# The up product of a two-layer MLP in seven block products instead of eight

## The chip, the cores and the metric

The program runs on one core of a Trainium2 chip. The core has TensorE (PE in the profile, with its weight loads as PEld), VectorE (DVE), ScalarE (ACT), GpSimd (POOL) and SyncE (SP, which issues the DMA transfers). The metric is the device time of one execution in microseconds (us). The kernel before took 2497.71 us, the median of three runs from 2495.82 to 2503.09.

## The reference

Two blocks of two layers each work on 512 tokens of 1024 features in float32. Only the second half of each layer of the first block is touched by the change:

```python
def hybrid_layer(x, ...):
    ...                                   # attention part
    x = x + mixed @ w_out
    h = rms_norm(x, mlp_norm_w)           # x / sqrt(mean(x^2) + eps) * mlp_norm_w
    return x + jnp.square(jax.nn.relu(h @ w_up)) @ w_down
```

`w_up` is 1024 x 4096 and `w_down` 4096 x 1024, one of each per layer; the first block has two layers. After it come a final norm and the second block (a forgetting attention, a linear recurrence and two gated MLPs), which stay as they are.

## The kernel before

Everything is held with features on the 128 partitions and the 512 tokens along the free axis: `x` is eight tiles of 128x512. A product in float32 accuracy is made of three matmuls in the rounded type fp32r (`mm3`, lines 321 to 323): each operand is split into a high part `hi`, which ScalarE makes by rounding, and a low part `lo`, the rest, which VectorE or GpSimd makes by subtraction; then hi x hi, hi x lo and lo x hi are added up in PSUM. A weight tile of 128 output features by 1024 input features comes by one DMA of 512 KB into a `raw` buffer (`load`, line 257), is rounded into `whi` (line 268) and subtracted into `wlo` (line 269). There are three buffers of each of the three. `fm_tiles` (line 329) makes one or more output tiles of 128x512: 8 chunks of the input x 3 matmuls of 512 columns, with the first six chunks of several tiles interleaved and the last two tile by tile.

The MLP (`mlp`, line 858) begins with `pre_norm`: the eight tiles `xg`, which are x times the norm's weight, split into high and low parts (lines 314, 315), and the squares of x (line 400) added up on VectorE (line 406). The factor 1/sqrt(mean square) of each token, `rstd`, is made on GpSimd (line 437), spread over the partitions as `rb`, and multiplied into the result of the up product rather than into its input. The squares take temporaries of the tag "t", of which there are four.

`up` makes the activation tiles: relu and the token's factor in one VectorE instruction out of PSUM (line 866), the square on ScalarE (867), the high part on ScalarE (275) and the low part on GpSimd (276). `down` makes the eight output tiles from eight activation tiles and adds them to x (874). A layer has 32 up tiles and 32 down products of eight chunks, in four groups of eight (`groups`, line 878): the first three up tiles together, five more, then for each group two up tiles of the next group, the eight down tiles, and six more up tiles.

The kernel is written in a framework that tracks dependencies and buffers. Each engine has one queue in a fixed order. The order is settled beforehand by a planner that gives every engine, by its own cost estimates, the first instruction in program order that is ready and has a free buffer; so an instruction can be moved ahead of ones written before it. The buffers of the MLP lie in a pool of their own, opened by `phase` in `hybrid`, over the addresses of the attention part.

Of the kernel before, what the change touches and what calls it, by code (L numbers as in the profile page):

```python
# [8 lines left out]
F = mybir.dt.float32  # L9
R = mybir.dt.float32r  # L10
B = mybir.dt.bfloat16
AF = mybir.ActivationFunctionType
OP = mybir.AluOpType
AX = mybir.AxisListType

S = 512
# [144 lines left out]
class Net:  # L161
# [183 lines left out]
    def catch_up(self):  # L345
# [2 lines left out]
            f()  # L348
        self.later = []

    def tm_half(self, ps, h, src, acts, width, low=None):


        if h == 0:
            ps = [self.mm_tile() for _ in range(NB)]
        w = self.weights(src, 4 * width, low)
        for tb in range(NB):
            ts = slice(tb * 128, (tb + 1) * 128)
            for k in range(4):
                sl = slice(k * width, (k + 1) * width)  # L360
                a = acts[4 * h + k]
                self.mm3(ps[tb][:, :width], (a[0][:, ts], a[1][:, ts]), (w[0][:, sl], w[1][:, sl]),
                         h == 0 and k == 0, h == 1 and k == 3)
        return ps
# [207 lines left out]
    def hybrid(self, l):  # L572
        with self.phase(act=10, lo=4, v=2, o=1, pr=2, ph=2, pl=2, score=1, gt=2):
            self.mixers(l)
        with self.phase(act=20):
            self.mlp(l)

    def mixers(self, l):
# [279 lines left out]
    def mlp(self, l):  # L858
        nc, I, x = self.nc, self.I, self.x
        xg, _, rb = self.pre_norm("mlp_norm", l)  # L860

        def up(js):
            out = []
            for ps in self.fm_tiles([(self.weights(I["w1up"][l, j], 1024, nc.vector), 0) for j in js], xg):
                t, s = self.temp(), self.temp()
                nc.vector.scalar_tensor_tensor(t, ps, 0.0, rb, op0=OP.max, op1=OP.mult)  # L866
                nc.scalar.activation(s, t, AF.Square)
                out.append(self.split(s, nc.gpsimd))
            return out

        def down(g, acts):
            for j in range(8):
                ps = self.fm_tile(self.weights(I["w1down"][l, g, j], 1024, nc.vector), acts)
                nc.vector.tensor_add(x[j], x[j], ps)  # L874

        self.groups([8] * 4, up, down)

    def groups(self, sizes, up, down, ahead=2, together=3):

# [410 lines left out]
```

## Time and profile before

| what | value |
|---|---|
| median of three runs | 2497.71 us |
| the profiled execution | 2494.83 us |
| its span | 2493.0 us |
| TensorE busy | 2404.7 us (96%), 11217 matmuls |
| VectorE, ScalarE, GpSimd busy | 1360.7 (55%), 1039.4 (42%), 619.0 (25%) us |
| granted TensorE clock, mean | 0.992 |
| DMA | 215.30 MB, mean 86 GB/s |

Busy time of TensorE is not the same as TensorE at its peak, as matmuls overlap: one of 512 columns is shown with some 0.4 us, while the next one starts some 0.23 us after it. The distance between starts is the better measure of what a matmul costs. The busy time of VectorE and GpSimd holds what an instruction waits for after it has started.

### The profile page before, as it was taken

How to read it: one execution, taken by the hardware profiler on the slowest of the kernel's cores; microseconds unless marked ns; L12 is line 12 of the kernel's file. 1: busy time of each engine (PE TensorE's matmuls, PEld its weight loads, DVE VectorE, ACT ScalarE, POOL GpSimd, SP SyncE). 2: the span in 40 equal slices, each digit the busy share in tenths (PEclk: the TensorE clock that was granted, in tenths of full speed). 3: DMA queues.
4: the chain of work that ended last, by engine and by line, in shares of the span. 5: the costliest groups of instructions: out<-in, count | busy, mean ns of one | idle time of the engine just before them, and what ended most of it. 6: DMA issues, size and time to landing. Idle time of an engine off the chain costs nothing.

```text
span 2493.0 us, 29049 instructions
## 1 busy us (share of the span) xinstructions
PE 2404.7 (96%) x11217; PEld 1950.8 (78%) x11217; DVE 1360.7 (55%) x2217; ACT 1039.4 (42%) x1625; POOL 619.0 (25%) x435
## 2 busy tenths in 40 slices
PE   9899999999998999999999999999999989999997
PEld 7787788888877878888887886888886766888886
DVE  6978643333488786333347867333336765433334
ACT  5656642232365675332233564223223563322222
POOL 3465320011045742110112531100001542100101
PEclk9999999999999999999999999999999999999998
DMA  4311132222232112222222211222222322322221
GB/s 160 106 64 47 64 102 93 95 100 93 77 104 91 60 47 86 100 93 93 93 97 77 84 52 60 97 98 94 93 83 70 95 75 68 102 96 98 94 87 66
DMA packets 61513, 215.30 MB, mean 86 GB/s; under 512 B 6848, under 2 KB 6976, under 8 KB 61376
## 3 DMA queue, kind: packets, MB, share of 16 engines
q1 hardware_dynamic: 59760, 207.06, 25.0%
q0 software_dynamic: 1472, 6.29, 0.7%
q8 instruction: 88, 1.44, 0.2%
q14 instruction: 49, 0.40, 0.1%
q10 hardware_dynamic: 144, 0.11, 0.0%
HBM read 211.33 MB, written 2.10 MB: 86 GB/s over the span
## 4 chain that ended last, share of the span: by engine, by line
PE 78%; DVE 14%; ACT 4%; issue 3%; POOL 1%; DMA 0%; ACTq 0%; DVEq 0%; POOLq 0%
PE mm L323 24%; PE mm L322 24%; PE mm L321 24%; DVE x L946 1%; DVE score L647 1%; PE st L307 1%; DVE m L646 1%; PE st L308 1%; PE st L542 1%; DVE m L1143 1%; ACT xg L314 1%; DVE act L287 1%; PE av L416 1%; DVE hs L1172 1%; PE av L491 1%
## 5 line engine op out<-in xcount | busy, mean ns | idle before, releaser
L268 ACT ACTIVATE whi<-raw 128x1024 fp32r<-128x1024 f32 (+3 forms) x398 | 409.8, 1032 | 1116.7 <-PE mm L322 934.6
L323 PE MATMUL mm<-xg,wlo 128*128 128x512 f32 x1792 | 711.5, 398 | 1.7 <-DVE wlo L269 1.7
L321 PE MATMUL mm<-xg,whi 128*128 128x512 f32 x1792 | 699.1, 394 | 14.3 <-ACT xg L314 12.1
L322 PE MATMUL mm<-xg,whi 128*128 128x512 f32 x1792 | 711.3, 397 | 0.2
L321 PE MATMUL mm<-act,whi 128*128 128x512 f32 x1160 | 455.8, 395 | 11.4 <-ACT act L275 8.5
L322 PE MATMUL mm<-act,whi 128*128 128x512 f32 x1160 | 459.8, 397 | 1.4 <-POOL act L276 1.4
L323 PE MATMUL mm<-act,wlo 128*128 128x512 f32 x1160 | 460.3, 397 | 0.0
L276 POOL TENSOR_TENSOR act<-t,act 128x512 fp32r<-128x512 f32 x108 | 150.4, 1395 | 1105.6 <-ACT act L275 1077.3
L269 DVE TENSOR_TENSOR wlo<-raw,whi 128x1024 fp32r<-128x1024 f32 (+2 forms) x289 | 348.4, 1207 | 135.8 <-ACT whi L268 135.3
L321 PEld LDWEIGHTS mm<-xg,whi 128*128 128x128 f32 x1792 | 339.5, 190 | 99.1 <-ACT xg L314 20.3
L322 PEld LDWEIGHTS mm<-xg,whi 128*128 128x128 f32 x1792 | 337.1, 188 | 82.9 <-DVE xg L315 6.6
L323 PEld LDWEIGHTS mm<-xg,wlo 128*128 128x128 f32 x1792 | 336.7, 188 | 76.2 <-DVE wlo L269 4.1
L269 POOL TENSOR_TENSOR wlo<-raw,whi 128x1024 fp32r<-128x1024 f32 (+3 forms) x109 | 257.3, 2362 | 296.0 <-ACT whi L268 284.7
L321 PEld LDWEIGHTS mm<-act,whi 128*128 128x128 f32 x1160 | 220.4, 190 | 64.6 <-ACT act L275 10.9
L322 PEld LDWEIGHTS mm<-act,whi 128*128 128x128 f32 x1160 | 218.3, 188 | 54.3 <-DVE act L276 2.3
L323 PEld LDWEIGHTS mm<-act,wlo 128*128 128x128 f32 x1160 | 218.1, 188 | 47.4
L874 DVE TENSOR_TENSOR x<-x,mm 128x512 f32<-128x512 f32 x64 | 44.0, 688 | 206.2 <-PE mm L323 206.2
L866 DVE SCALAR_TENSOR_TENSOR t<-mm,rb 128x512 f32<-128x512 f32 x64 | 44.1, 691 | 198.8 <-PE mm L323 198.6
L1237 DVE TENSOR_TENSOR t<-mm,rb 128x512 f32<-128x512 f32 x44 | 30.4, 691 | 141.8 <-PE mm L323 141.8
L1235 DVE TENSOR_TENSOR t<-mm,rb 128x512 f32<-128x512 f32 x44 | 30.4, 691 | 118.1 <-PE mm L323 118.1
L275 ACT ACTIVATE act<-t 128x512 fp32r<-128x512 f32 x114 | 72.1, 633 | 50.2 <-DVE t L1238 32.9
L307 PE MATMUL st<-act,act 128*128 128x128 f32 (+3 forms) x208 | 72.2, 356 | 20.8 <-DVE act L287 8.8
(226 smaller groups left out, 2641.5 us busy)
## 6 DMA issues: line engine op xcount, KB each, us to landing
raw<-in_w1up SPq DMA_DIRECT2D x64, 512.0 KB, 3.3
raw<-in_w1down SPq DMA_DIRECT2D x64, 512.0 KB, 3.2
raw<-in_gate SPq DMA_DIRECT2D x44, 512.0 KB, 3.3
raw<-in_up SPq DMA_DIRECT2D x44, 512.0 KB, 3.2
raw<-in_w1fm SPq DMA_DIRECT2D x41, 512.0 KB, 3.3
raw<-in_down SPq DMA_DIRECT2D x32, 512.0 KB, 3.2
raw<-in_odin SPq DMA_DIRECT2D x16, 512.0 KB, 3.3
raw<-in_w1out SPq DMA_DIRECT2D x16, 384.0 KB, 3.0
```

The costliest lines, as they stand in the source:

```text
L268: nc.scalar.activation(hi[:, sl], raw[:, sl], AF.Copy)
L269: (low or nc.gpsimd).tensor_sub(lo[:, sl], raw[:, sl], hi[:, sl].bitcast(F))
L275: nc.scalar.activation(hi, t, AF.Copy)
L276: (low or nc.vector).tensor_sub(lo, t, hi.bitcast(F))
L307: mm(ps, a[:, rows], b[hh][:, cols], start=True, stop=False, skip_group_check=True)
L321: mm(ps, w[0], a[0], start=first, stop=False, skip_group_check=True)
L322: mm(ps, w[0], a[1], start=False, stop=False, skip_group_check=True)
L323: self.last_mm = mm(ps, w[1], a[0], start=False, stop=last, skip_group_check=True)
L866: nc.vector.scalar_tensor_tensor(t, ps, 0.0, rb, op0=OP.max, op1=OP.mult)
L874: nc.vector.tensor_add(x[j], x[j], ps)
L1235: nc.vector.tensor_mul(t, pg, rb)
L1237: nc.vector.tensor_mul(u, pu, rb)
```

## The change

In the MLPs of the first block, 26 of the 32 up tiles of a layer are made in 13 pairs. A pair is 256 output features by 512 tokens by 1024 inputs. It is cut in two along each of the three: the features (two tiles), the inputs (chunks 0 to 3 and 4 to 7) and the tokens (0 to 255 and 256 to 511). The product of two 2x2 block matrices is formed of seven block products and a number of block sums, where the plain way has eight. The sums of token blocks (`token_sums`) are made once a layer, those of weight blocks (`pair_weights`) once a pair, both on GpSimd, and both are split into high and low parts as other operands are. A block product is 4 chunks x 3 matmuls of 256 columns. `seven` runs in three parts: three products, then two, then two; the last part of a pair is put behind the first part of the next pair, or behind the first down tile. Two of the PSUM tiles are read after the first part and are added to further. What follows the up product (relu, factor, square, split) is done for the two tiles of a pair from SBUF. Tiles 0 to 3, 30 and 31 are made as before.

The pool of the MLP holds 10 activation tiles in place of 20, and the tiles of the sums. The descriptor memory for transfers that GpSimd issues is halved.

```diff
+    def token_sums(self, x, g):
+        nc, out = self.nc, []
+        for k in range(4):
+            b = [self.temp() for _ in range(2)]
+            for i in range(2):
+                nc.scalar.activation(b[i], x[k + 4 * i], AF.Copy, scale=g(k + 4 * i))
+            (b11, b12), (b21, b22) = [(t[:, :256], t[:, 256:]) for t in b]
+            f = self.get("sum", 2 * S)
+            t1, t2, t3, t4 = [f[:, 256 * i:256 * i + 256] for i in range(4)]
+            nc.gpsimd.tensor_sub(t1, b12, b11)
+            nc.gpsimd.tensor_sub(t2, b22, t1)
+            nc.gpsimd.tensor_sub(t3, b22, b12)
+            nc.gpsimd.tensor_sub(t4, b21, t2)
+            t = self.get("tok", 4 * S, R)
+            hi, lo = t[:, :2 * S], t[:, 2 * S:]
+            nc.scalar.activation(hi, f, AF.Copy)
+            nc.vector.tensor_sub(lo, f, hi.bitcast(F))
+            out.append((hi, lo))
+        return out
+
+    def pair_weights(self, src):
+        nc = self.nc
+        r0, r1 = (self.load(a, 1024) for a in src)
+        (a11, a12), (a21, a22) = [(r[:, :S], r[:, S:2 * S]) for r in (r0, r1)]
+        def parts(t, width, tags):
...
+            nc.scalar.activation(hi[:, :width], t, AF.Copy)
+            nc.vector.tensor_sub(lo[:, :width], t, hi[:, :width].bitcast(F))
+            return hi, lo
+        a1 = parts(r0[:, :1024], 1024, ("whi", "wlo"))
+        p, q = self.get("sum", 2 * S), self.get("sum", 2 * S)
+        s1, s2, s3, s4 = p[:, :S], p[:, S:], q[:, :S], q[:, S:]
+        nc.gpsimd.tensor_add(s1, a21, a22)
+        nc.gpsimd.tensor_sub(s2, s1, a11)
+        s12 = parts(p, 1024, ("shi", "slo"))
+        nc.gpsimd.tensor_sub(s3, a11, a21)
+        nc.gpsimd.tensor_sub(s4, a12, s2)
+        s34 = parts(q, 1024, ("shi", "slo"))
+        a2 = parts(a22, 512, ("whi", "wlo"))
+        return a1, s12, s34, a2
+
+    def seven(self, src, xg, tok, post):
...
+        def product(ps, w, j, b, first):
+            for k in range(4):
+                sl = slice(512 * j + 128 * k, 512 * j + 128 * k + 128)
+                self.mm3(ps, (w[0][:, sl], w[1][:, sl]), b(k), first and k == 0, k == 3)
+        p1, p2, p3 = (t[:, :256] for t in (self.mm_tile(), self.mm_tile(), self.st_tile()))
...
+        product(p1, a1, 0, plain(0, 0), True)
+        product(p2, s12, 1, summed(1), True)
+        product(p3, s12, 0, summed(0), True)
+        nc.scalar.activation(r1, p1, AF.Copy)
+        nc.vector.tensor_add(r2, p2, r1)
+        yield
+        t, u = self.temp(), self.temp()
+        product(p1, a1, 1, plain(1, 0), False)
+        product(p2, s34, 0, summed(2), False)
+        nc.scalar.activation(t[:, half[0]], p1, AF.Copy)
+        nc.vector.tensor_add(r3, p2, r1)
+        nc.vector.tensor_add(u[:, half[1]], p3, r3)
+        yield
+        product(p2, a2, 0, summed(3), False)
+        product(p3, s34, 1, plain(1, 1), False)
+        nc.vector.tensor_add(u[:, half[0]], p2, r1)
+        nc.vector.tensor_add(t[:, half[1]], p3, r2)
+        post(t, u)
+        yield
...
-        with self.phase(act=20):
+        with self.phase(act=10, tok=4, sum=2, shi=3, slo=3, r=2):
             self.mlp(l)
...
+        def both(j):
+            def post(*tu):
+                for i, t in enumerate(tu):
+                    nc.vector.scalar_tensor_tensor(t, t, 0.0, rb, op0=OP.max, op1=OP.mult)
+                    nc.scalar.activation(t, t, AF.Square)
+                    acts[j + i] = self.split(t, nc.gpsimd)
+            return self.seven([I["w1up"][l, j + i] for i in range(2)], xg, tok, post)
...
+        def pairs(js):
+            for j in js:
+                now = both(j)
+                next(now)
+                finish()
+                next(now)
+                left.append(now)
+
+        def finish():
+            while left:
+                next(left.pop())
+
+        up(range(3))
+        tok = self.token_sums(x, lambda c: self.v("mlp_norm", 8 * l + c))
+        up([3])
+        pairs([4, 6])
+        for g in range(4):
+            if g < 3:
+                pairs([8 * g + 8])
+            down(g, 0)
+            finish()
+            for j in range(1, 8):
+                down(g, j)
+            if g < 2:
+                pairs(range(8 * g + 10, 8 * g + 16, 2))
+            elif g == 2:
+                pairs([26, 28])
+                up([30])
+                finish()
+                up([31])
...
-    nc = _bacc.Bacc("TRN2", target_bir_lowering=False, num_devices=1, dynamic_dma_scratch_size=8192)
+    nc = _bacc.Bacc("TRN2", target_bir_lowering=False, num_devices=1, dynamic_dma_scratch_size=4096)
```

## Rows read from the trace of the kernel before

**Rows 1.** The page: busy time by engine, and the chain that ended last.
```profile
PE 2404.7 (96%) x11217; PEld 1950.8 (78%) x11217; DVE 1360.7 (55%) x2217; ACT 1039.4 (42%) x1625; POOL 619.0 (25%) x435
...
PE 78%; DVE 14%; ACT 4%; issue 3%; POOL 1%; DMA 0%; ACTq 0%; DVEq 0%; POOLq 0%
```

**Rows 2.** Windows: length, busy by engine (instructions), clock, DMA share, GB/s.
```profile
180.00:240.00 60.00, 55.71 (x295) 45.49 (x293) 52.45 (x132) 42.00 (x87) 34.39 (x28) 1.00 0.13 43
340.00:660.00 320.00, 320.00 (x1381) 260.26 (x1380) 117.14 (x126) 101.46 (x125) 38.27 (x32) 1.00 0.28 94
```

**Rows 3.** Waits from 309 to 666 us: total us, times, longest.
```profile
ACT whi L268 <- PE mm L322: 217.8, 58, 8.2
...
DVE t L866 <- PE mm L323: 99.3, 29, 3.5
```

**Rows 4.** Timeline, TensorE: first matmul of one up tile and of the next.
```profile
411.18 0.39 PE L321 MATMUL mm<-xg,whi 128*128 128x512 f32 x1
...
416.73 0.39 PE L321 MATMUL mm<-xg,whi 128*128 128x512 f32 x1
```

**Rows 5.** Timeline, TensorE: matmuls of 256 columns, 43 starts apart.
```profile
159.96 0.28 PE L323 MATMUL mm<-whi,xg 128*128 128x256 f32 x1
...
164.99 0.28 PE L321 MATMUL mm<-whi,xg 128*128 128x256 f32 x1
```

**Rows 6.** Groups by form, VectorE: count, busy us, mean ns, idle before.
```profile
L269 DVE TENSOR_TENSOR wlo<-raw,whi 128x1024 fp32r<-128x1024 f32 x264 | 324.4, 1230 | 123.1 <-ACT whi L268 122.6
...
L1238 DVE TENSOR_TENSOR t<-t,t 128x512 f32<-128x512 f32 x44 | 30.4, 692 | 5.6 <-ACT t L1236 1.7
...
L547 DVE TENSOR_TENSOR pl<-st,ph 128x256 fp32r<-128x256 f32 x32 | 13.2, 413 | 1.8 <-ACT ph L546 1.8
```

**Rows 7.** Groups by form, ScalarE.
```profile
L268 ACT ACTIVATE whi<-raw 128x1024 fp32r<-128x1024 f32 x351 | 371.1, 1059 | 1031.5 <-PE mm L322 874.4 <-issue 138.8 <-PE mm L323 6.5
...
L867 ACT ACTIVATE t<-t 128x512 f32<-128x512 f32 x64 | 40.4, 632 | 2.8 <-DVE t L866 2.5 <-issue 0.2
...
L546 ACT ACTIVATE ph<-st 128x256 fp32r<-128x256 f32 x32 | 12.3, 385 | 0.0
```

**Rows 8.** Groups by form, GpSimd.
```profile
L406 POOL TENSOR_TENSOR acc<-acc,t 128x512 f32<-128x512 f32 x15 | 19.5, 1299 | 42.0 <-ACT t L400 42.0
...
L276 POOL TENSOR_TENSOR pl<-t,ph 128x256 fp32r<-128x256 f32 x8 | 7.0, 876 | 11.9 <-ACT ph L275 11.7
```

**Rows 9.** Timeline, VectorE and GpSimd: an add alone and beside GpSimd.
```profile
2097.65 0.68 DVE L946 TENSOR_TENSOR x<-x,m 128x512 f32<-128x512 f32 x1
2103.04 1.80 DVE L946 TENSOR_TENSOR x<-x,m 128x512 f32<-128x512 f32 x1
2103.00 1.29 POOL L406 TENSOR_TENSOR acc<-acc,t 128x512 f32<-128x512 f32 x1 [1.97 <-ACT t L400]
```

**Rows 10.** Timeline, VectorE and GpSimd, at the first layer's MLP start.
```profile
316.23 3.08 DVE L406 TENSOR_TENSOR acc<-acc,t 128x512 f32<-128x512 f32 x4
...
333.46 0.69 DVE L866 SCALAR_TENSOR_TENSOR t<-mm,rb 128x512 f32<-128x512 f32 x1 [2.25 <-PE mm L323]
320.97 1.04 POOL L437 TENSOR_TENSOR rstd<-var,mhalf 128x4 f32<-128x4 f32 x1 [26.12 <-DVE var L422]
331.23 3.81 POOL L276 TENSOR_TENSOR act<-t,act 128x512 fp32r<-128x512 f32 x3 [9.23 <-ACT act L275]
```

**Rows 11.** Windows and TensorE's timeline around one idle time (clock third from last).
```profile
128.00:134.00 6.00, 5.56 (x26) 5.57 (x27) 5.49 (x12) 2.30 (x5) 1.38 (x2) 0.50 0.26 90
...
128.44 1.11 PE L719 MATMUL st<-const_sb,t 128*128 128x128 f32 x4 [3.38 <-DVE t L713]
```

**Rows 12.** DMA issues: a transfer that GpSimd issues (count, KB, us to landing).
```profile
pr<-in_decay POOLq DMA_DIRECT2D x8, 640.0 KB, 4.7
```

More of the change, by code (lines that the diff above doesn't have):

```diff
@@ new lines, in pair_weights @@
+    def pair_weights(self, src):
[3 more added lines that the diff above has]
+        def parts(t, width, tags):
+            pool = self.wp if tags[0] == "whi" else self.pool
+            kw = {} if tags[0] == "whi" else {"bufs": self.bufs[tags[0]]}
+            w = 1056 if tags[0] == "whi" else 1024
+            hi, lo = (pool.tile([128, w], R, tag=tag, name=self.name(tag), **kw) for tag in tags)
+            nc.scalar.activation(hi[:, :width], t, AF.Copy)
[12 more added lines that the diff above has]
+        return a1, s12, s34, a2
@@ new lines, in seven, with plain, summed @@
+    def seven(self, src, xg, tok, post):
+        nc = self.nc
+        a1, s12, s34, a2 = self.pair_weights(src)
+        half = (slice(0, 256), slice(256, 512))
+        def plain(j, i):
+            return lambda k: tuple(part[:, half[i]] for part in xg[4 * j + k])
+        def summed(i):
+            return lambda k: tuple(part[:, 256 * i:256 * i + 256] for part in tok[k])
+        def product(ps, w, j, b, first):
[3 more added lines that the diff above has]
+        p1, p2, p3 = (t[:, :256] for t in (self.mm_tile(), self.mm_tile(), self.st_tile()))
+        r = self.get("r", 768)
+        r1, r2, r3 = (r[:, 256 * i:256 * i + 256] for i in range(3))
+        product(p1, a1, 0, plain(0, 0), True)
[17 more added lines that the diff above has]
+        yield
@@ L860, in mlp @@
         xg, _, rb = self.pre_norm("mlp_norm", l)
-        def up(js):
[L863 to L874, printed above, removed]
@@ L876, in mlp, with squared @@
-        self.groups([8] * 4, up, down)
+        acts = {}
+        def squared(j, ps):
+            t = self.temp()
+            nc.vector.scalar_tensor_tensor(t, ps, 0.0, rb, op0=OP.max, op1=OP.mult)
+            nc.scalar.activation(t, t, AF.Square)
+            acts[j] = self.split(t, nc.gpsimd)
+        def up(js):
+            for j, ps in zip(js, self.fm_tiles([(self.weights(I["w1up"][l, j], 1024, nc.vector), 0) for j in js], xg)):
+                squared(j, ps)
+        def both(j):
+            def post(*tu):
+                for i, t in enumerate(tu):
+                    nc.vector.scalar_tensor_tensor(t, t, 0.0, rb, op0=OP.max, op1=OP.mult)
+                    nc.scalar.activation(t, t, AF.Square)
+                    acts[j + i] = self.split(t, nc.gpsimd)
+            return self.seven([I["w1up"][l, j + i] for i in range(2)], xg, tok, post)
@@ new lines, in down @@
+        def down(g, j):
+            ps = self.fm_tile(self.weights(I["w1down"][l, g, j], 1024, nc.vector), [acts[8 * g + k] for k in range(8)])
+            nc.vector.tensor_add(x[j], x[j], ps)
+        left = []
+        def pairs(js):
[9 more added lines that the diff above has]
+        up(range(3))
```

## The prediction

> **What bounds the kernel now.** I read the page's busy times and its chain first, then the MLP stage by windows, then the waits in it, then single instructions. The reader is to see that TensorE is busy for 96% of the span and makes 78% of the chain that ended last [rows 1]. In the MLP stage of the first layer TensorE is busy for 320.00 of 320 us at full clock, while VectorE works 117, ScalarE 101 and GpSimd 38 of them [rows 2]. The waits agree: there ScalarE's weight copies wait for TensorE to release a weight buffer, 58 times and 218 us in all, and VectorE's evacuations wait for the last matmul of their tile [rows 3]; TensorE has no wait in this stage. So a matmul column taken away here shortens the time until another engine fills its place, and the whole question is how far the three others, at 12 to 37% now, can be loaded.
>
> **The matmuls.** A tile of the up product is 8 chunks x 3 matmuls of 512 columns. One tile's 24 matmuls start 411.18 to 416.73, 5.55 us, 231 ns each [rows 4]; a pair of tiles costs 11.10 us. In the new form a pair is 7 products x 4 chunks x 3 matmuls = 84, of 256 columns. The trace has that pattern already, twelve matmuls of 256 columns to a bank, each with its own 128x128 weight load, in the value projections of the mixers: 43 starts from 159.96 to 164.99 [rows 5] are 117.0 ns each, hardly over half of 231. That makes 84 x 0.117 = 9.83 us, 1.27 us less a pair, and over 13 pairs x 2 layers **33.1 us less**. The new products have the weights stationary and tokens moving, those of the row the other way round; shapes and types are the same, so I take the price unchanged.
>
> The Trainium skill (TensorE: Matmul & The Clock Gate, section Back-to-back issue gap) gives 518 cycles for 512 columns and 262 for 256. By those figures, as an estimate, the saving would be 30.9 us; the trace's pitches are longer, 231 and 117 ns, and they decide.
>
> **What is added per pair.** By the forms of [rows 6 to 8]:
> - ScalarE: three 1024-wide roundings at 1.059 in place of two, and a 512-wide one at 0.632; two 256-wide copies out of PSUM at 0.385; the four squares and roundings at 0.632 stay. 7.1 us of 9.83 (before 4.6 of 11.10).
> - VectorE: three 1024-wide subtractions at 1.23, one of 512 at 0.69, five 256-wide adds out of PSUM at 0.413, two relu-scalings at 0.692. 7.8 us (before 3.8).
> - GpSimd: four 512-wide weight sums at 1.30 and the two low parts at 1.27 (3.81 for three [rows 10]). 7.7 us (before 2.5).
>
> Each alone fits beside 9.83 us of matmuls. Together they fit less well, because GpSimd and VectorE exclude each other in some instructions: the add x + m takes 0.68 alone and 1.80 when it starts 0.04 us after a 1.29 us GpSimd add [rows 9], about the rest of that and its own time. Only VectorE instructions with both operands in SBUF meet this; the evacuation beside a GpSimd one keeps its 0.69 [rows 10]. Per pair the instructions that exclude each other are GpSimd's 7.7 and VectorE's subtractions and relu-scalings, 4.4 + 1.4: **13.5 us against 9.83**. That is no bound by itself, as pairs come in stretches of four (10, 12, 14, 16) between eight down tiles of 5.55 us, whose only such work is one subtraction of 1.23. In those the buffers let the first pair's weights be made whole (5.2 + 4.4) and the second's sums and first rounding (5.2 + 1.2), 16.0 us ahead. Of the stretch's 54 us, 16.0 are thus done and 4.0 (the last pair's relu and low parts) come after it: 34 us fall in 39.3 us of matmuls. It fits with an eighth to spare, with queues in a fixed order. The cost of the collisions lies between nothing (the 0 of the MLP stage, VectorE at 37%) and the 7.1% that TensorE stands idle at 180 to 240 us, where VectorE is busy at 87% [rows 2]: 0 to 0.70 us a pair, 18 us in all at the upper end. That stretch is attention, where TensorE hangs on VectorE inside each head, while here a weight buffer lies ready ahead; I take 0.25, **6.5 us over 26 pairs**.
>
> **The beginning of each layer's MLP.** Here nothing can be done ahead. The token sums need all of x, and their scaled copies take the four "t" temporaries that the squares of the norm still hold: those are released by the adds that end at 316.23 + 3.08 = 319.3 [rows 10], the first about 317, so GpSimd can begin at about 318. From there the work of GpSimd, and of VectorE where it excludes GpSimd, before the first pair's second product is: 16 subtractions of 128x256, between half of 1.27 and the 0.876 of that form [rows 8], taken as 0.75, 12.0 us; their four low parts at 1.23, 4.9; the rstd power on GpSimd, 1.0 [rows 10]; the low parts of tile 3's and the pair's own weights, 2.5; s1 and s2, 2.6. That is 23.0, to 341.0, and then a rounding and a subtraction, 2.3: 343.3. TensorE leaves tile 3 at 333.46 [rows 10] and has one product of 1.4 us without sums, so it stands at 334.9, 8.4 us early. The scheduler can bring forward products of plain tokens, the pair's other one and one of the next pair, 2.8 us; 5.6 us of idling remain. One idle of 3.38 us in this trace dropped the granted clock to 0.50, the 1.2 GHz level, through 128 to 134 us [rows 11], where a 256-column matmul then needs twice the time: some 2.8 us more. Together 8.4 us a layer, **16.8 us for two**. Ends: 0, if the sums hide; 8.4 + 3.8 + 2.8 = 15.0, if the first three tiles' low parts (3.81, GpSimd) stand before the sums and nothing is brought forward.
>
> **Edits costed at nothing.** r2, r3 and the halves are read out of PSUM while other products run: after part one of a pair comes the previous pair's last part (2.8 us) or a product of a1, against 0.41 or 0.39 for the read; without that cover 0.4 to 0.8 us once a group. The first down tile after a pair needs that pair's two activations at its chunks 6 and 7, 2.8 + 18 x 0.231 = 7.0 us after the pair's last matmul; add, relu 0.69 twice, square and two roundings 0.63, low part 1.27 twice are 5.3 us; without cover up to 2 us, 6 times. The weight loads (two a pair, as before) wait on SP for a raw buffer, now held for four sums: 5.2 us, inside the pair's 9.83. Half the descriptor memory of the GpSimd queue touches 12 transfers in the mixers, 8 of them of 640 KB that land in 4.7 us [rows 12]. If each of the 8 waited for the one before it and all stood on the path, that would be 38 us; I take nothing, since no wait of TensorE in the profile is on them and they are few in the air at once.
>
> **Sum.** -33.1 + 6.5 + 16.8 = -9.8 us. The profiled execution took 2494.83 us (span 2493.0, 1.8 around it): 2485.0. It lies 2.9 below the median of the three runs; from that it would be 2487.9. I forecast 2486.
>
> **Rivals.**
> - *All of it hides* (22%). For it: GpSimd is idle for 26.1 us before 320.97 [rows 10]; the two sum engines may take their work in another order than I walked. Against: the temporaries. Start 0 to 2 us a layer and 0.1 us a pair: -33.1 + 4 = -29, 2466.
> - *The start eats it* (20%). The low parts of tiles 0 to 2 are older work and stand ahead of the sums, and the clock falls: 15 us a layer. -33.1 + 30 + 6.5 = +3, 2498.
> - *The shared access becomes the bound in the stretches* (15%, slower). Place: the four-pair stretches; price 13.5 us a pair instead of 9.83. With no work ahead, 26 x (13.5 - 11.10) = +62. If half of the 16 us in each of six stretches is had ahead, +62 - 48 + 16.8 = +31, 2526. It decides from 9.83 + (33.1 - 16.8) / 26 = 10.5 us a pair. For it: whi, shi and raw have three buffers and a pair takes two of each, so work ahead may be little. Against: the walk above. The Trainium skill (SBUF — State Buffer, Who interferes with whom) has this rule: a VectorE instruction with two SBUF inputs and a GpSimd one that reads SBUF hold a shared access by turns, whole instructions long, and the second to come is blocked fully. The trace agrees by the 1.80 against 0.68.
> - *256 columns cost more here* (3%). A pair breaks even at 11.10 / 84 = 132 ns a matmul; the row says 117.
>
> **How the numbers follow.** My own case has 40%, at 2486, from 2478 to 2494. This kernel's timing can tell 0.3%, 7.5 us, from no change: under 2490 is faster, over 2505 slower. Faster: 22 + 35 of my 40 = 57%. Same: 17 of the start's 20, 5 of mine and 3 of the third rival's 15, 25%. Slower: the other 12, the fourth's 3 and 3 of the start's, 18%. The range takes the first rival nearly whole and leaves out the worse half of the third: 2463 to 2508.
>
> **What would show it.** The 256-column matmuls of the up product start 117 ns apart in a stretch, and one layer's stage shortens by 16.5 less its idling. TensorE's waits gain a line at the first pair of each layer, on the low part of the first weight sums, 5 to 12 us, with a clock of 0.50 after it. GpSimd rises to about 120 us a layer, and VectorE's subtractions average over 1.4 us where they meet it. I am wrong if TensorE waits more than 0.6 us a pair inside the stretches, or if the start has no such wait.

## The result, and the profile after

The changed kernel takes 2538.68 us (median of four runs, 2531.17 to 2540.32) against 2500.40 for the kernel before beside it: a ratio of **1.0149, 95% interval 1.0122 to 1.0176**. It is slower by 1.5%, and 31 us above the upper end of my range.

From here on each layer's MLP is cut at three marks: the last of the attention part's adds to x, the first down product's add to x, and the last one. These rows give them for the first layer, first of the kernel before, then of the changed one (line, engine, operation, output and inputs, count: shortest/median/longest ns, first and last start).

```profile
L856 DVE TENSOR_TENSOR x<-x,mm x8: 681/682/687, 301.8 to 309.5; 128x512 f32<-128x512 f32 x8
L874 DVE TENSOR_TENSOR x<-x,mm x32: 686/687/689, 372.4 to 667.5; 128x512 f32<-128x512 f32 x32
```

```profile
L948 DVE TENSOR_TENSOR x<-x,mm x8: 681/685/689, 302.3 to 310.0; 128x512 f32<-128x512 f32 x8
L975 DVE TENSOR_TENSOR x<-x,mm x32: 673/686/690, 394.3 to 685.8; 128x512 f32<-128x512 f32 x32
```

The *start* (first mark to second) was 372.4 - 309.5 = 62.9 us and is 84.3. The *body* (second to third) was 295.1 and is 291.5. The second layer gives the same: 63.0 and 295.1 before, 84.4 and 292.8 after. So the bodies are 5.9 us shorter in all and the starts 42.8 longer. The profiled executions differ by 45.3 us (span 2538.3 against 2493.0); the rest is the attention part of the second layer, 309.4 against 301.3. Its code is the same, and over the profiled executions of this study it took 299.5 to 309.4, so I don't count it to the change; the 309.4 itself stays unexplained.

The page after, answering to [rows 1]: busy times, then the chain of waits by engine. TensorE's share of the chain has fallen from 78% to 71% and GpSimd's risen from 1% to 4%; GpSimd's busy time is 181 us longer.

```profile
PE 2393.1 (94%) x12153; PEld 1987.9 (78%) x12153; DVE 1480.7 (58%) x2407; ACT 1108.0 (44%) x1753; POOL 800.1 (32%) x571
PE 71%; DVE 15%; issue 4%; ACT 4%; POOL 4%; DMA 1%; SPq 0%; POOLq 0%; ACTq 0%; DVEq 0%
```

TensorE's waits in the first layer's MLP, 310 to 690 us (engine, line, releaser: us in total, times, longest). In the kernel before this view is empty.

```profile
PE mm L321 <- ACT r L426: 17.0, 1, 17.0
PE mm L323 <- DVE wlo L387: 3.4, 2, 1.7
PE mm L321 <- ACT shi L386: 2.5, 2, 2.3
PE mm L321 <- DVE r L427: 2.1, 1, 2.1
PE mm L323 <- DVE slo L387: 0.8, 1, 0.8
```

The second line lies in the body, the other four, 22.4 us, at the start. Windows of TensorE there (stretch, PE busy and count, granted clock, DMA share, GB/s):

```profile
330.00:340.00 10.00, 5.31 (x29) 0.89 0.00 1
340.00:350.00 10.00, 0.00 (x0) 0.50 0.00 0
350.00:360.00 10.00, 7.48 (x39) 0.59 0.06 10
360.00:370.00 10.00, 4.81 (x31) 0.92 0.55 187
370.00:380.00 10.00, 10.00 (x79) 0.90 0.16 50
```

TensorE stands still from 335.3 to 352.3. When it starts again the clock is at 0.50, the 1.2 GHz level, and the 256-column matmuls come 0.21 us apart instead of 0.12; over the whole start that, and the first matmul behind each wait, is some 5 us more. The next three fences show the standstill: GpSimd, ScalarE and TensorE of the changed kernel (start, us, instruction, [idle before it and what ended it]).

```profile
321.49 1.04 POOL L529 TENSOR_TENSOR rstd<-var,mhalf 128x4 f32<-128x4 f32 x1 [26.12 <-DVE var L514]
330.98 0.74 POOL L363 TENSOR_TENSOR sum<-t 128x256 f32<-128x256 f32 x1 [8.45 <-ACT t L359]
331.68 3.92 POOL L276 TENSOR_TENSOR act<-t,act 128x512 fp32r<-128x512 f32 x3
335.55 0.73 POOL L364 TENSOR_TENSOR sum<-t,sum 128x256 f32<-128x256 f32 x1
...
349.68 0.72 POOL L366 TENSOR_TENSOR sum<-t,sum 128x256 f32<-128x256 f32 x1
350.36 1.27 POOL L393 TENSOR_TENSOR sum<-raw 128x512 f32<-128x512 f32 x1
```

```profile
324.58 1.06 ACT L268 ACTIVATE whi<-raw 128x1024 fp32r<-128x1024 f32 x1 [8.15 <-PE mm L322]
...
330.20 0.71 ACT L359 ACTIVATE t<-x,vec_sb 128x512 f32<-128x512 f32 x1
...
334.39 0.73 ACT L359 ACTIVATE t<-x,vec_sb 128x512 f32<-128x512 f32 x1 [0.27 <-POOL act L276]
...
346.60 1.06 ACT L369 ACTIVATE tok<-sum 128x1024 fp32r<-128x1024 f32 x1 [1.59 <-POOL sum L366]
350.43 1.06 ACT L369 ACTIVATE tok<-sum 128x1024 fp32r<-128x1024 f32 x1 [2.77 <-POOL sum L366]
351.39 0.61 ACT L958 ACTIVATE t<-t 128x512 f32<-128x512 f32 x1
351.91 0.36 ACT L426 ACTIVATE r<-mm 128x256 f32<-128x256 f32 x1
```

```profile
352.33 0.58 PE L321 MATMUL mm<-xg,whi 128*128 128x256 f32 x1 [17.02 <-ACT r L426]
```

Read them in this order. GpSimd is free from 322.5, and waits 8.45 us for the first scaled copy of x (line 359), which ScalarE makes only at 330.20. The copy needs a temporary "t". All four were free by 319.8, when the norm's last add ends, but a tag's buffers are handed out in the order of the program, and the results of tiles 0 to 2 (`up(range(3))`) are written ahead of the copies: three of the four went to them, and those can't be filled before rb exists. The copy at 334.39 says it: it waits for a low part of an activation (line 276), which frees a temporary. The first copy has the fourth temporary and waits for no buffer. It stands in ScalarE's queue behind a weight rounding that waited 8.15 us for TensorE (324.58), behind rb and behind a first square; why the planner put it there the trace doesn't show. GpSimd makes the three low parts of tiles 0 to 2 (3.92) in between, then the sums until 350.4. ScalarE, in its fixed order, waits for them four times, and behind those waits stands the read of the pair's first product, r1 (line 426, 0.36 us), on which TensorE waits.

The 17.0 us are not what r1 costs, though. The first matmul with a token sum starts at 355.03, only 2.7 us after TensorE goes on, so an earlier r1 would have moved the standstill more than shortened it. The chain that ended last doesn't pass through r1; it stays with GpSimd for most of the time from 330.98 to 366. Pieces of it (start, us, what):

```profile
330.98 0.74 POOL sum L363
...
341.50 1.06 ACT tok L369
342.56 0.62 ACT t L359
343.25 1.17 POOL sum L363
...
356.13 2.22 POOL sum L396
358.37 3.44 DMA raw<-in_w1up
361.98 1.28 POOL sum L393
```

At its end GpSimd waits for the weights of the next pair, whose load starts only when a buffer that the sums read is free.

### The profile page after: what moved, and what is told of

It is laid out like the page before. It is cut to its first block, busy times and chain, and to the rows that moved or that the text cites. A ratio compares the mean times of both kernels' runs of the same rounds, so it can differ in the third digit from the quotient of the medians.

```text
span 2538.3 us, 31459 instructions
## 1 busy us (share of the span) xinstructions
PE 2393.1 (94%) x12153; PEld 1987.9 (78%) x12153; DVE 1480.7 (58%) x2407; ACT 1108.0 (44%) x1753; POOL 800.1 (32%) x571
## 4 chain that ended last, share of the span: by engine, by line
PE 71%; DVE 15%; issue 4%; ACT 4%; POOL 4%; DMA 1%; SPq 0%; POOLq 0%; ACTq 0%; DVEq 0%
PE mm L323 21%; PE mm L322 21%; PE mm L321 21%; DVE x L1078 1%; PE st L307 1%; DVE score L739 1%; PE st L308 1%; DMA raw<-in_w1up 1%; DVE m L738 1%; POOL act L276 1%; DVE m L1275 1%; PE st L634 1%; DVE act L287 1%; PE st L321 1%; PE st L322 1%
## 5 line engine op out<-in xcount | busy, mean ns | idle before, releaser
L268 ACT ACTIVATE whi<-raw 128x1024 fp32r<-128x1024 f32 (+3 forms) x346 | 354.8, 1028 | 872.7 <-PE mm L322 681.1
L321 PE MATMUL mm<-xg,whi 128*128 128x512 f32 (+1 forms) x1584 | 598.6, 383 | 47.4 <-ACT r L426 34.0
L323 PE MATMUL mm<-xg,wlo 128*128 128x512 f32 (+1 forms) x1584 | 607.7, 384 | 9.2 <-DVE wlo L387 7.1
L322 PE MATMUL mm<-xg,whi 128*128 128x512 f32 (+1 forms) x1584 | 608.0, 384 | 0.2
L276 POOL TENSOR_TENSOR act<-t,act 128x512 fp32r<-128x512 f32 x108 | 155.9, 1453 | 758.1 <-ACT act L275 738.3
L321 PEld LDWEIGHTS mm<-xg,whi 128*128 128x128 f32 x1584 | 301.9, 192 | 114.9 <-ACT r L426 34.6
L269 DVE TENSOR_TENSOR wlo<-raw,whi 128x1024 fp32r<-128x1024 f32 (+3 forms) x237 | 286.8, 1212 | 127.4 <-ACT whi L268 126.8
L323 PEld LDWEIGHTS mm<-xg,wlo 128*128 128x128 f32 x1584 | 300.2, 190 | 67.8 <-DVE wlo L387 7.9
L322 PEld LDWEIGHTS mm<-xg,whi 128*128 128x128 f32 x1584 | 300.6, 190 | 64.8 <-DVE xg L315 6.7
L321 PEld LDWEIGHTS mm<-act,whi 128*128 128x128 f32 x1160 | 220.4, 191 | 62.7 <-ACT act L275 10.5
L387 DVE TENSOR_TENSOR slo<-sum,shi 128x1024 fp32r<-128x1024 f32 x52 | 69.1, 1330 | 111.6 <-ACT shi L386 106.1
L386 ACT ACTIVATE shi<-sum 128x1024 fp32r<-128x1024 f32 x52 | 55.2, 1061 | 137.2 <-POOL sum L394 110.4
L529 POOL TENSOR_TENSOR rstd<-var,mhalf 128x4 f32<-128x4 f32 x14 | 14.9, 1068 | 272.4 <-DVE var L514 272.4
```

The source lines that it names most:

```text
L268: nc.scalar.activation(hi[:, sl], raw[:, sl], AF.Copy)
L269: (low or nc.gpsimd).tensor_sub(lo[:, sl], raw[:, sl], hi[:, sl].bitcast(F))
L276: (low or nc.vector).tensor_sub(lo, t, hi.bitcast(F))
L321: mm(ps, w[0], a[0], start=first, stop=False, skip_group_check=True)
L322: mm(ps, w[0], a[1], start=False, stop=False, skip_group_check=True)
L323: self.last_mm = mm(ps, w[1], a[0], start=False, stop=last, skip_group_check=True)
```

## The experiments

Theory: the order of the queues at the start makes the loss. First rival: the sums are too much work wherever they stand. The table has all runs, starts and bodies of both layers from the marks above.

| kernel | start | body | median us | ratio to before (95%) |
|---|---|---|---|---|
| before | 62.9, 63.0 | 295.1, 295.1 | | |
| the change | 84.3, 84.4 | 291.5, 292.8 | 2538.68 | 1.0149 (1.0122 to 1.0176) |
| before, less descriptor memory | 62.9, 63.0 | 295.2, 295.1 | 2497.45 | 1.0004 (0.9991 to 1.0017) |
| own buffers for the copies | 74.5, 73.7 | 293.2, 294.2 | 2515.28 | 1.0064 (1.0040 to 1.0088) |
| token sums first | 76.0, 76.0 | 291.5, 291.8 | 2515.61 | 1.0066 (1.0045 to 1.0087) |
| no token sums | 66.3, 65.6 | 294.6, 291.7 | 2499.93 | 1.0007 (0.9993 to 1.0022) |
| no sums at all | 56.7, 56.8 | 287.0, 286.9 | 2474.69 | 0.9908 (0.9881 to 0.9936) |
| six plain tiles first | 78.5, 78.8 | 293.4, 293.9 | 2528.24 | 1.0123 (1.0094 to 1.0152) |
| eight plain tiles first | 72.0, 71.8 | 291.1, 292.1 | 2511.27 | 1.0054 (1.0038 to 1.0071) |
| a pair's own weights first | 84.7, 84.7 | 288.7, 288.6 | 2527.67 | 1.0118 (1.0096 to 1.0140) |
| eight plain, sums last | 65.5, 65.6 | 288.5, 288.4 | 2488.96 | 0.9964 (0.9951 to 0.9977) |
| six plain, sums last | 77.3, 76.1 | 288.6, 288.8 | 2512.70 | 1.0054 (1.0036 to 1.0072) |
| four plain, sums last | 78.3, 78.4 | 288.8, 288.8 | 2516.54 | 1.0071 (1.0056 to 1.0086) |
| six plain, sums last, read first | 71.8, 71.2 | 288.6, 288.7 | 2505.96 | 1.0025 (1.0012 to 1.0037) |

For starts with fewer pairs, what they would be without a wait is an estimate from the rows: of the ten up tiles ahead of the first down product the change makes six in three pairs, and the last of these pairs leaves its last part, 24 matmuls, for later. A plain tile is 295.1 / 53 = 5.57 us (22 up and 31 down tiles in the body), a matmul of a pair 0.119. Six plain tiles out, 33.4, and 228 matmuls in, 27.1: 62.9 - 6.3 = 56.6, against 56.7 measured without sums. With six plain tiles first it is 57.7 (144 matmuls in), with eight 58.9 (60 in).

**The descriptor memory alone.**

```diff
-    nc = _bacc.Bacc("TRN2", ..., dynamic_dma_scratch_size=8192)
+    nc = _bacc.Bacc("TRN2", ..., dynamic_dma_scratch_size=4096)
```

> The kernel before with only the descriptor memory of GpSimd's transfers halved, as the change has it. Theory A (the attention part of the second layer took 7.3 us longer after the change because transfers that GpSimd issues land later): 2500 becomes 2505 to 2515, and from the end of the first layer's MLP to the first up tile of the second it takes about 328 us instead of 321. Theory B (it comes from where the new order puts things in time, or from the clock): 2500 as before, 321 us.

Measured: 2497.45 us, 1.0004. It costs nothing that can be told, as costed. The attention part of the second layer took 304.4 us here, between the 301.3 and the 309.4, so this run doesn't settle where that difference comes from.

**Own buffers for the scaled copies, and the sums ahead of the first tiles.** Two ways to give GpSimd its work at 318.

```diff
-            b = [self.temp() for _ in range(2)]
+            b = [self.get("r", 768)[:, :S] for _ in range(2)]
```

> The changed kernel, but the scaled copies of x for the token sums lie in the buffers of r (free until the first pair) instead of the four temporaries t. Theory 1 (the copies stand behind the evacuations of tiles 0 to 2, because the planner hands out the t temporaries in the order of the program, so the sums begin at 330 us instead of about 312): the sums begin before 320 us, TensorE's 17 us wait at the first pair of each layer shrinks to under 8, and the time falls by 20 us a layer, from 2539 to about 2500. Theory 2 (the amount of work of GpSimd and VectorE at the start is what costs, wherever it begins): the wait stays over 12 us and the time over 2525.

```diff
-        up(range(3))
         tok = self.token_sums(x, lambda c: self.v("mlp_norm", 8 * l + c))
+        up(range(3))
```

> The changed kernel with the token sums written ahead of tiles 0 to 2 in the program, with the four t temporaries as they are. Theory 1 (order of the temporaries and of GpSimd's queue): the sums begin at about 318 us, when the squares of the norm release t, and are done before the low parts of tiles 0 to 2; the wait at the first pair falls below 8 us and the time to 2500 or less. Theory 2 (amount of work): as now, over 2525, since the evacuations of tiles 0 to 2 then wait for the temporaries instead.

Measured: 2515.28 and 2515.61 us. Counted from the attention part's last add, the first sum started 3.3 and 8.3 us after it, against 21.0 in the change, and the start became 8 to 11 us shorter a layer. But 17 to 19 of the 28 us stayed, more than the theory in this form allowed. With own buffers the copies now stood ahead of the norm's squares on ScalarE and the sums ahead of the norm's power on GpSimd, so rb was made 29.9 us after that add instead of 18.3 and the evacuations waited; TensorE waited 4.4 us for the norm's sum and 6.0 for r1. With the sums first, a plain tile's weights were caught; ScalarE of that kernel:

```profile
335.57 1.06 ACT L369 ACTIVATE tok<-sum 128x1024 fp32r<-128x1024 f32 x1 [2.77 <-POOL sum L366]
336.53 1.04 ACT L268 ACTIVATE whi<-raw 128x1024 fp32r<-128x1024 f32 x1
```

That rounding of tile 3's weights (line 268) was what TensorE waited 8.7 us for. So the buffers are one cause (they are the only edit of the first run), and taking it away moves part of the loss to the next thing in a queue.

**No token sums.** The products that take a token sum read a half of the plain tokens in its place. With the sums go their eight scaled copies, four roundings and four low parts a layer; nothing else is left out.

```diff
-        tok = self.token_sums(x, lambda c: self.v("mlp_norm", 8 * l + c))
+        tok = None
...
-            return lambda k: tuple(part[:, 256 * i:256 * i + 256] for part in tok[k])
+            return lambda k: tuple(part[:, half[i % 2]] for part in xg[k])
```

> The changed kernel without the token sums: products that take a sum of tokens take a plain half of the tokens instead (the up product is then not the reference's); weight sums and all else stay. It bounds what the token sums cost. Theory 1 and theory 2 both give the start back here: the first pair waits under 4 us for its weight sums, the first down tile is added at about 368 us instead of 394, and the time is 2539 - 2 x 25 = about 2489. If it stays over 2515, the weight sums and the collisions of the pairs are the cost, not the token sums.

Measured: 2499.93 us, between the two. The start is 66.0, 18 less than in the change and still 9 over its 56.7: TensorE waited 5.0 us for r1 again, which stood behind the second pair's rounding of weight sums.

**No sums at all.**

```diff
-        nc.gpsimd.tensor_add(s1, a21, a22)
-        nc.gpsimd.tensor_sub(s2, s1, a11)
-        s12 = parts(p, 1024, ("shi", "slo"))
-        nc.gpsimd.tensor_sub(s3, a11, a21)
-        nc.gpsimd.tensor_sub(s4, a12, s2)
-        s34 = parts(q, 1024, ("shi", "slo"))
+        s12 = parts(r0[:, :1024], 1024, ("shi", "slo"))
+        s34 = parts(r1[:, :1024], 1024, ("shi", "slo"))
```

> Neither token sums nor weight sums are formed: the products that take a sum read the plain tokens or the raw weights in its place, so the up product is another one; all matmuls, roundings, subtractions and PSUM reads stay. GpSimd has the low parts of the activations alone. Theory (what is left of the loss without token sums, 10 us a layer at the start and 6 to 9 in the stretches, comes from the weight sums on GpSimd: queues stand behind them, and VectorE's subtractions are blocked by them): start loss under 3 us a layer, the two waits of 1.7 us a layer on the low part of a pair's own weights gone, 2496 - 28 + about 6 = 2474. Rival (three buffers of the rounded weights and the queues' order, not GpSimd): waits and start stay, 2490 to 2500.

Measured: 2474.69 us, as the theory had it. TensorE has no wait from 300 to 700 us, the clock stays at 1.00, and all matmuls and each pair's roundings, subtractions and reads of PSUM are there as in the change. What the expectation passed over: the token sums' copies and roundings on ScalarE, some 10 us a layer, and their four low parts on VectorE are gone as well. Windows of TensorE in this kernel over the same stretch as above:

```profile
340.00:350.00 10.00, 10.00 (x86) 1.00 0.33 107
350.00:360.00 10.00, 10.00 (x86) 1.00 0.33 105
```

So what the change loses comes by way of the sums: the weight sums are GpSimd's alone, and for the token sums this run can't part GpSimd's work from ScalarE's. By difference, of the 27.6 us a layer at the start, 18.4 need the token sums (84.35 - 66.0) and 9.2 the weight sums; of the body's 291.5 to 292.8, 4.5 to 5.9 are theirs.

**More plain tiles first, in the change's order.**

```diff
         up([3])
-        pairs([4, 6])
+        up([4])
+        up([5])
+        pairs([6])
```

> Two more plain up tiles at the start of each layer: tiles 0 to 5 plain, 12 pairs, all else as in the change, the order of the sums too. A pair saves 1.09 us as the change's stretches show it (11.14 against 84 x 0.1196), so 12 pairs x 2 save 26 us. Theory (the sums at the start are a fixed amount of work on GpSimd and ScalarE that lacks cover): two plain tiles give 11 us of cover, and the 28 us that a layer loses at its start fall to about 17; with the 8 us of waits in the stretches the time is about 2496 - 26 + 34 + 8 = 2512. Rival (the planner's order of temporaries decides, and moves with the evacuations): the sums are put back behind the two added evacuations as well, the loss stays at 25 to 28 a layer, and the time is 2530 or more.

```diff
-        up([3])
-        pairs([4, 6])
+        for j in range(3, 8):
+            up([j])
```

> Eight plain up tiles at the start of each layer and 11 pairs: the token sums and the first pair's weight sums have 22 us of plain matmuls more to hide behind than in the change. 11 pairs x 2 x 1.09 save 24 us. Theory (fixed work that lacks cover): the loss at the start falls from 28 to 0 to 6 us a layer; with 8 us of waits in the stretches 2496 - 24 + 0 to 12 + 8 = 2480 to 2492. Rival (order decides): the loss stays above 15 a layer, 2510 or more.

Measured: 2528.24 and 2511.27 us. Both lie nearer to the rival (order decides) without meeting it in full: the losses are 21 and 13 us a layer, where the theory had 17 and 0 to 6 and the rival 25 to 28 and over 15. Twenty-two us more of matmuls don't hide the sums, because the plain tiles' own weights stand behind them (with six plain tiles it is the first pair's own weights, for the same 10.4 us). TensorE of the kernel with eight plain tiles:

```profile
355.89 0.79 PE L321 MATMUL mm<-xg,whi 128*128 128x512 f32 x1 [10.41 <-ACT whi L268]
```

and ScalarE ahead of it: the last token rounding, which had waited 2.78 for GpSimd, two squares and two roundings that had piled up, and then the weights that TensorE wanted at 345.5.

```profile
351.76 1.06 ACT L369 ACTIVATE tok<-sum 128x1024 fp32r<-128x1024 f32 x1 [2.78 <-POOL sum L366]
352.72 1.13 ACT L958 ACTIVATE t<-t 128x512 f32<-128x512 f32 x2
353.76 1.13 ACT L275 ACTIVATE act<-t 128x512 fp32r<-128x512 f32 x2
354.80 1.99 ACT L268 ACTIVATE whi<-raw 128x1024 fp32r<-128x1024 f32 x2
```

**A pair's own weights first.** The body's two waits of 1.7 us. ScalarE, VectorE and TensorE of the change around one of them: the rounding of a1 (461.90) stands behind that of the weight sums (460.93, which waited 4.70 us for GpSimd), its subtraction (463.50) behind theirs (462.03).

```profile
460.93 1.06 ACT L386 ACTIVATE shi<-sum 128x1024 fp32r<-128x1024 f32 x1 [4.70 <-POOL sum L394]
461.90 1.04 ACT L386 ACTIVATE whi<-raw 128x1024 fp32r<-128x1024 f32 x1
```

```profile
462.03 1.23 DVE L387 TENSOR_TENSOR slo<-sum,shi 128x1024 fp32r<-128x1024 f32 x1 [5.12 <-PE mm L322]
463.50 1.96 DVE L387 TENSOR_TENSOR wlo<-raw,whi 128x1024 fp32r<-128x1024 f32 x1
```

```profile
465.52 0.38 PE L323 MATMUL mm<-xg,wlo 128*128 128x256 f32 x1 [1.74 <-DVE wlo L387]
```

```diff
-            nc.scalar.activation(hi[:, :width], t, AF.Copy)
-            nc.vector.tensor_sub(lo[:, :width], t, hi[:, :width].bitcast(F))
+            ab = [nc.scalar.activation(hi[:, :width], t, AF.Copy),
+                  nc.vector.tensor_sub(lo[:, :width], t, hi[:, :width].bitcast(F))]
+            for own, other in zip(ab, ahead):
+                self.after(own, other)
+            ahead[:] = ab
```

> The change with the order of a pair's four roundings on ScalarE and of its four subtractions on VectorE pinned to that of the program: a pair's own weights (a1) before its first weight sums, then the second sums, then a2. In the change a1 stands behind the sums' rounding, which waits for GpSimd. Theory: TensorE's waits on the low part of a1 (2 a layer, 2.0 us each between matmul starts) go, 8 us less, and the start stays: about 2530. Rival (a1 waits for its buffer, freed by the last part of the pair before the last): the waits stay, within 3 us of the change, 2536 or more.

Measured: 2527.67 us. The body's waits on wlo are gone, in the first layer's body TensorE waits 1.0 us in all, and the bodies are 288.7 and 288.6 (2.8 and 4.2 less); the starts are as they were. The theory holds for the place. The median fell by 11.0, of which 7.0 are the bodies; in the profiled executions the rest lies in the second layer's attention part (302.2 against 309.4).

**The order turned round.** The token sums written behind the plain tiles, their copies in own buffers, behind the norm's squares on ScalarE and behind its power on GpSimd, with a pair's own weights first; n is eight, six and four plain tiles, `self.square` the norm's last square and `self.root` its power.

```diff
+        for j in range(3, n):
+            up([j])
         tok = self.token_sums(x, lambda c: self.v("mlp_norm", 8 * l + c))
-        up([3])
-        pairs([4, 6])
+        pairs(range(n, 8, 2))
...
+                self.after(nc.scalar.activation(b[i], x[k + 4 * i], AF.Copy, scale=g(k + 4 * i)), self.square)
...
+            self.after(nc.gpsimd.tensor_sub(t1, b12, b11), self.root)
```

> Eight plain up tiles first and 11 pairs; the token sums are written behind the plain tiles, so that in the planner's order plain work goes first on each engine; their scaled copies take buffers of their own and stand behind the norm's last square on ScalarE and behind the norm's power on GpSimd; a pair's roundings and subtractions are in the program's order. Theory (the loss was one of order: rounding and reads that TensorE needs stood in ScalarE's queue behind roundings that wait for GpSimd): the end of the mixers to the first down tile is 58.5 us if nothing waits, and I expect at most 3 more (72.0 with eight plain tiles and the change's order); first to last down tile 288.7 as with the pinned pair: 2496.5 + 2 x (58.5 + 1.5 - 62.9) + 2 x (288.7 - 295.1) = 2478, within 2474 to 2484, and faster than the kernel before. Rival (the token sums' work delays whatever their place): over 2490.

> The same with six plain up tiles first and 12 pairs. Without waits the start is 57.4 us. Theory of order: GpSimd's sums run from 322 and end by about 340, TensorE needs them at about 346, so at most 5 us are lost a layer: 2496.5 + 2 x (57.4 + 0 to 5 - 62.9) - 12.8 = 2473 to 2483. Rival: over 2490.

> The same with four plain up tiles first and 13 pairs, as many as in the change. Without waits the start is 56.4 us; the change took 84.4. Theory of order: what remains is the work that can't be had earlier, 16 sums, three low parts and two weight sums on GpSimd from 322 on, to about 343, against TensorE at 336, with a drop of the clock: 8 to 12 us a layer, so 2496.5 + 2 x (56.4 + 10 - 62.9) - 12.8 = 2491 (2486 to 2496). Rival (the amount of sum work sets the loss): 2505 or more.

Measured: 2488.96, 2512.70 and 2516.54 us. With eight plain tiles the start falls from 72 to 65.5, 7 over its 58.9, and the kernel is **faster than the one before, 0.9964 (0.9951 to 0.9977)**, though by 9 us where I had expected 18. With six and four the rival was right: 19 and 22 us a layer stay. So with the first pair close behind the norm, none of the orders tried does it. With six plain tiles, two things are to be seen, on ScalarE and TensorE:

```profile
351.50 1.06 ACT L386 ACTIVATE shi<-sum 128x1024 fp32r<-128x1024 f32 x1 [2.41 <-POOL sum L398]
...
363.58 1.06 ACT L386 ACTIVATE shi<-sum 128x1024 fp32r<-128x1024 f32 x1 [3.32 <-POOL sum L398]
364.54 0.61 ACT L275 ACTIVATE act<-t 128x512 fp32r<-128x512 f32 x1
365.06 0.36 ACT L430 ACTIVATE r<-mm 128x256 f32<-128x256 f32 x1
```

```profile
365.48 0.58 PE L321 MATMUL mm<-xg,whi 128*128 128x256 f32 x1 [6.88 <-ACT r L430]
```

The first sums come late (TensorE waits 5.3 us for the rounding at 351.50: GpSimd has low parts to make in between, and stood idle for 4.3 us before 334.31 because ScalarE made a scaled copy only behind two weight roundings and rb), and then r1 is read behind the second pair's rounding at 363.58.

**The reads ahead of the next pair's rounding.**

```diff
-        nc.scalar.activation(r1, p1, AF.Copy)
-        nc.vector.tensor_add(r2, p2, r1)
+        self.reads = [nc.scalar.activation(r1, p1, AF.Copy), nc.vector.tensor_add(r2, p2, r1)]
...
         s12 = parts(p, 1024, ("shi", "slo"))
+        for own, other in zip(ahead, self.reads):
+            self.after(own, other)
```

> The kernel with six plain tiles and the sums last, with one thing more: the first weight sums of a pair are rounded on ScalarE, and subtracted on VectorE, only behind the two reads (r1, r2) of the pair before it. In the run without it TensorE waited 6.9 us a layer for r1 (ready at about 356, read at 365.06), which stood behind the second pair's rounding, and that waited for GpSimd; the clock was 0.57 after it. Theory (a small read that TensorE needs is caught in an in-order queue): the 6.9 us go, some 2 us come back as a wait on the second pair's sums, and the clock recovers: the start falls from 77 to 68 to 72 us, 2512.7 - 2 x 5 to 9 = 2495 to 2503. Rival (GpSimd's sums are late for TensorE anyway and the read only hides it): the wait moves to the second pair's sums in full, start over 75, 2508 or more.

Measured: 2505.96 us. The wait for r1 went from 6.9 to 2.3 us, the start from 77.3 and 76.1 to 71.8 and 71.2, within what the theory gave for it; the median lies between the two expectations. What is left is the wait for the first sums, 5.4 us, the clock (0.69 from 360 to 370) and the 2.3 for r1, which now stands on ScalarE behind a square that waits 1.60 us for VectorE.

## Why the prediction was wrong

**The step that failed: "The beginning of each layer's MLP".** I gave it 8.4 us a layer, 16.8 in all, with 15.0 a layer as the upper end. It lost 84.35 - 56.75 = 27.6 a layer against the same products without sums, 55 in all: 38 us of a miss of 55 in the profiled execution (the rest is 4 of matmuls, 4 of collisions and order in the bodies, and the 8 of the attention part). The 16 subtractions were sized well: they take 0.72 to 0.74 each where VectorE leaves them alone (taken as 0.75). From GpSimd's first sum to the first matmul with a token sum it is 330.98 to 355.03, 24.1 us; I had 25.3, but that is partly luck: I had put the sums' four low parts, the norm's power and two weights' low parts into it, some 8 us in a row, and the trace has in their place three low parts of activations (3.92), a wait of GpSimd for ScalarE (1.78) and sums that VectorE held up. What was wrong first is where it begins, 318 in place of 331. I had looked when the four temporaries are free, and not who gets them: I wrote that the planner takes the first ready instruction in program order, but didn't apply it to the buffers, so the evacuations of three tiles that are ready only after rb held three of the four. Wrong second are the 2.8 us of plain products that were to be brought forward: TensorE stopped at 335.3, after the first product, because the next one needs r1 and the next pair's needs weights that were rounded at 352.69, both behind the token sums' roundings on ScalarE. My rival "The start eats it" had the low parts ahead of the sums and the clock right (3.92 us, 0.50), and stopped at 15 a layer for the same reason.

Even that is not the whole. With the sums begun as early as I had put them, the start still lost 17 to 19, and I had asked only when GpSimd ends. Between GpSimd and TensorE stands ScalarE, in a fixed order, and while it waits for a sum, all that TensorE needs from it waits too: a plain tile's weights (8.7 and 10.4 us), r1 (6.9 and 5.0), rb. I had called it 7.1 of 9.83 us and no bound. Its busy time says nothing about this.

**The matmuls.** Right in kind, small in size: without sums the starts and bodies are 2 x (6.2 + 8.15) = 28.7 us shorter instead of 33.1. In the body, 287.0 less 33 plain tiles of 5.57 is 103.2 us for 864 matmuls, 119 ns each; the row I took had 117 [rows 5]. That is 4.4 us of the miss.

**Collisions.** Taken as 6.5. The bodies of the change are 10.4 us longer than without sums; 7.0 of these go when a pair's own weights come first, and were order again; 3.4 stay, at most, for collisions. VectorE's subtractions do meet GpSimd: in the body's wait above one takes 1.96 us, where without sums they take 1.22; a sum of GpSimd runs beside it until 464.39, and the subtraction ends 1.1 us later. The rule of the Trainium skill (SBUF — State Buffer, Who interferes with whom), that one of the two is blocked for the other's whole instruction, agrees with this. But over the some 20 pairs of the two bodies the 3.4 are at most a sixth of a microsecond a pair. The rival of a bound by shared access is out: a pair takes some 10.5 us in the change's bodies, not 13.5, and TensorE waits 0.3 to 0.4 us a pair there, under the 0.6 that I had named.

**The signs.** The wait at each layer's first pair and the clock of 0.50 came, the wait longer (17.0 us for 5 to 12) and on another thing, r1. GpSimd is busy 135.9 us from 310 to 690 (named: about 120).

**Edits at nothing.** The descriptor memory and the first down tile cost nothing that shows, as put, and the reads r2 and r3 inside the body at most 0.5 us a layer. The weight loads did show: the chain that ended last has one of 3.44 us at the first layer's start (above) and five of 3.4 to 3.6 in the second layer. What they cost by themselves no run shows. The read r1 I had not listed at all; in the kernel without token sums TensorE waits 5.0 us for it, and putting it first in the kernel with six plain tiles shortened the start by 5.

**What stays open.** How far the start can be brought down with four plain tiles first: the best of the orders tried left 17 us a layer. How much of a late token sum is GpSimd's own work and how much ScalarE's copies and roundings for it was not separated. Low parts of the activations behind the sums on GpSimd, and the token roundings on another engine than ScalarE, were not tried. The 7 us a layer that the best kernel still loses are 2.6 of waiting for r1, 1.0 for weights' low parts, and for the rest I have only its clock (0.88 from 360 to 370).

## What to carry to other kernels

Where new work feeds an engine through another one with a fixed order, don't ask only how long it takes: walk the queue of the engine in between, and list everything that the bound engine needs from it behind each new wait. In this framework buffers shared by tag go out in program order, so new users written behind old ones wait until the old ones are through, even when the buffers are free. A saving of one part in eight needs cover at its beginning: give the preparation some tiles of the old form to hide behind, and write it behind them. Here it took eight such tiles; in the change, with four, the starts lost 55 us, and all the pairs save 28.7.

## What the runs showed that I had not expected

Matmuls of 256 columns, each with a weight load of its own, keep 119 ns over whole stretches, 52% of the 231 of 512 columns [rows 4]. A standstill of 17.0 us left the clock at 0.50 when TensorE began again and at 0.59 in the mean of that window: 22.4 us of waits at the start went with a loss of 27.6.
